# Declaring away the waits that other waits already imply, in a kernel that sums reciprocals

## The chip, the cores and the metric

The kernel runs on one core of one Trainium2 chip. The metric is the device time of one execution in microseconds (us). The input is 64 MiB of float32 in HBM, the output 64 KiB.

## The reference

```python
def setup_inputs():
    batch, seq, dim = 32, 512, 1024
    return {"x": np.abs(np.random.randn(batch, seq, dim)).astype(np.float32) + 1e-6}

def reference(x):
    return np.sum(1.0 / x, axis=-1).astype(np.float32)
```

There are 16384 rows of 1024 positive numbers. For each row the sum of the reciprocals is wanted.

## The kernel before

The 16384 rows are spread over the 128 partitions, 128 rows on each. In what follows "row r" (0 to 127) means row r of every partition at once: a block of 128 x 1024 numbers, 512 KB.

A reciprocal is taken as exp(-ln(v)) on ScalarE. To halve that work, the kernel splits a row into two halves a and b of 512 and takes only one reciprocal for each pair, q = 1/(a*b). Then 1/a + 1/b = (a + b) * q. A plan written out by hand, a list of tokens (PLAN), gives the order of all work; `tc.manual_schedule()` keeps each engine's instructions in that order. A token is a letter, a row, a count of rows (+2) and a place (@6):

- **D** (line 120): SyncE issues a load of the next n rows into the ring, a buffer in SBUF for 40 rows. There are 32 loads, the first nine of 8 rows, the last nine of one row. Loads take eight semaphores in turn.
- **P** (line 129): GpSimd multiplies the halves of one to three rows into a slot of `prod` (22 slots).
- **C** and **V** (lines 138 and 143): in place of P, TensorE copies the second half into a bank of PSUM with an identity matrix, and VectorE multiplies the halves. **W** (line 143) is the same product on VectorE with both halves read from SBUF.
- **S** (line 150): TensorE adds the halves into a PSUM bank, two matmuls with the identity, that the profile shows as four records.
- **L** (line 159): ScalarE takes ln of the slots, in place.
- **E** (line 167): ScalarE takes exp(-...), either in place in `prod` or into one or two PSUM banks (@).
- **R** (line 175): VectorE reduces. Where the row had an S, it multiplies q in `prod` (512) with the sum in PSUM and adds up. Otherwise it multiplies the row in the ring (1024) with q in PSUM, taken for both halves. A second, short instruction (DVE_READ_ACCUMULATOR2_ANT) writes the row's sum into `sums`.

At the end (line 195) SyncE stores `sums`.

The framework watches which instruction reads and writes which part of `ring`, `prod`, `ps` and `sums`, and sets semaphore waits for each dependence between engines. It knows what an engine has itself waited for, but not what that other engine had waited for before. An instruction carries one wait; further ones go into separate instructions in front of it on the same engine, which only wait (EVENT_SEMAPHORE in the profile). For example the reduce of row 0 waits for ScalarE, which wrote q into PSUM, and for GpSimd, which had read the row from the ring that the reduce overwrites. ScalarE had waited for GpSimd already, through `prod`.

The plan's last rows stand in this order: `S121@3 W121 R115 L119+3 P122 R118 S120@1 R117 E119+3 P123 R116 S124@4 L122+2 P124 R121 R120 E122+2 W125 S125@2 R119 L124+2 P126 R123 S126@0 E124+2 P127 R122 L126 R125 S127@1 E126 R124 L127 R126 E127 R127` (places left out where they do not matter). A little before come W117 and P118, neither of which needs the other.

Of the kernel before, what the change touches and what calls it, by code (L numbers as in the profile page):

```python
# [11 lines left out]
def kernel(  # L12
# [5 lines left out]
    nc = tc.nc  # L18
# [5 lines left out]
    R = 40  # L24
    NP = 22
    S = float(2**17)
# [41 lines left out]
    Ln = mybir.ActivationFunctionType.Ln  # L68
    Exp = mybir.ActivationFunctionType.Exp
# [34 lines left out]
    pslot = {r + j: b + j for op, r, n, b in ops if op == "L" for j in range(n)}  # L104

    def xs(r, h):
        return ring[:, r % R, h * H : (h + 1) * H]

    loaded = 0
    bank, copied, halves = {}, {}, set()  # L110

    with tc.manual_schedule():
        for op, r, n, b in ops:
            p = pslot.get(r)
            if op == "D":
                n, r = r, loaded
                while n:
                    a = r % R
                    m = min(n, R - a)  # L119
                    nc.sync.dma_start(  # L120
                        out=ring[:, a : a + m, :], in_=x_v[:, r : r + m, :]
                    )  # L122
                    r, n = r + m, n - m
                loaded = r  # L124
            elif op == "P":
                while n:  # L126
                    a, p = r % R, pslot[r]  # L127
                    m = min(n, R - a)
                    nc.gpsimd.tensor_tensor(  # L129
                        out=prod[:, p : p + m, :],  # L130
                        in0=ring[:, a : a + m, :H],
                        in1=ring[:, a : a + m, H:],
                        op=mult,
                    )
                    r, n = r + m, n - m
            elif op == "C":
                copied[r] = b
                nc.tensor.matmul(  # L138
                    ps[:, b, :], lhsT=ident, rhs=xs(r, 1), start=True, stop=True
                )  # L140
            elif op in "WV":
                in1 = xs(r, 1) if op == "W" else ps[:, copied[r], :]
                nc.vector.tensor_tensor(  # L143
                    out=prod[:, p, :], in0=xs(r, 0), in1=in1, op=mult
                )
            elif op == "S":
                bank[r] = b
                halves.add(r)
                for h in range(2):
                    nc.tensor.matmul(  # L150
                        ps[:, b, :],
                        lhsT=ident,
                        rhs=xs(r, h),
                        start=h == 0,
                        stop=h == 1,
                    )
            elif op == "L":
                pg = prod[:, p : p + n, :]
                nc.scalar.activation(out=pg, in_=pg, func=Ln, scale=S)  # L159
            elif op == "E":  # L160
                pg = prod[:, p : p + n, :]
                rc = pg
                if b is not None:
                    rc = ps[:, b : b + n, :]
                    for j in range(n):
                        bank[r + j] = b + j
                nc.scalar.activation(out=rc, in_=pg, func=Exp, scale=-1.0)  # L167
            elif op == "R":
                other = ps[:, bank[r], :]
                if r in halves:  # L170
                    row = prod[:, p, :]
                else:
                    row = ring[:, r % R, :].rearrange("p (h e) -> p h e", h=2)
                    other = other.unsqueeze(1).to_broadcast([P, 2, H])
                nc.vector.tensor_tensor_reduce(  # L175
                    out=row,
                    in0=row,
                    in1=other,
                    scale=S,
                    scalar=0.0,  # L180
                    op0=mult,
                    op1=add,
                    accum_out=sums[:, r : r + 1],
                )
            elif op == "X":
                row = ring[:, r % R, :]
                nc.scalar.activation(out=row, in_=row, func=Ln)
                nc.scalar.activation(
                    out=row,
                    in_=row,  # L190
                    func=Exp,
                    scale=-1.0,
                    accum_out=sums[:, r : r + 1],
                )
        nc.sync.dma_start(out=out_v, in_=sums)


# [28 lines left out]
```

## Time and profile before

| what | value |
|---|---|
| time, median of 4 runs | 171.75 us (171.58 to 172.11) |
| the profiled execution | 172.11 us, its span 170.1 us |
| TensorE matmul busy | 138.5 us (81%) |
| ScalarE busy | 131.1 us (77%) |
| VectorE busy | 130.4 us (77%) |
| GpSimd busy | 124.3 us (73%) |
| queue of the loads, share of 16 DMA engines over the span | 93.4% |
| read from HBM | 67.11 MB, 395 GB/s over the span |
| clock granted to TensorE, mean | 0.976 |

The span runs from the first to the last recorded instruction; the time of an execution also has what lies around it. In the profile's views L120 is line 120 of the kernel; PE is TensorE, PEld its weight loads, DVE is VectorE, ACT ScalarE, POOL GpSimd, SP SyncE, and a q behind the name (DVEq) is the engine's sequencer, that is its waiting instructions. The DMA view names each queue with its packets, megabytes and share; "instruction" packets are those that bring instructions to the engines.

### The profile page before, as it was taken

The page shows a single profiled execution, that of the slowest core. Times are in us where ns is not written, and L with a number is a line of the kernel's source. Part 1 is how long each engine was busy: PE and PEld are TensorE (multiplying, and loading weights), DVE is VectorE, ACT ScalarE, POOL GpSimd, SP SyncE. Part 2 cuts the span into 40 slices and gives each one's busy share as a digit, 9 for nine tenths or more (in the row PEclk, how much of TensorE's full clock was granted, in tenths as well). Part 3 has the DMA queues.
Part 4 walks back from the last instruction along what each step waited for, and adds up shares of the span by engine and source line. Part 5 has one row for each costly group of instructions (what it writes and reads, how often), then busy time and mean ns, then how long its engine had stood idle before and what let it go on. Part 6 is the DMA issues. An engine that isn't in the chain of part 4 may idle for free.

```text
span 170.1 us, 1382 instructions
## 1 busy us (share of the span) xinstructions
PE 138.5 (81%) x300; PEld 57.9 (34%) x300; DVE 130.4 (77%) x281; ACT 131.1 (77%) x133; POOL 124.3 (73%) x73
## 2 busy tenths in 40 slices
PE   0008999796995989779995999859999999898990
PEld 0003444242432434234342443224443444333340
DVE  0001777868886886868868689999999999999991
ACT  3002969969595996949789699988987999896990
POOL 1008969697995969779696999959919876974750
PEclk9999999999997899969999999999999999999998
DMA  6999999999999999999999999999999999999600
GB/s 216 401 470 393 462 401 447 416 447 416 424 433 424 439 424 435 433 432 439 424 439 405 418 420 433 443 409 424 435 416 428 420 425 427 408 409 408 252 4 17
DMA packets 4760, 67.26 MB, mean 395 GB/s; under 512 B 528, under 2 KB 656, under 8 KB 1808
## 3 DMA queue, kind: packets, MB, share of 16 engines
q1 hardware_dynamic: 4752, 67.18, 93.4%
q14 instruction: 6, 0.05, 0.1%
q8 instruction: 2, 0.03, 0.1%
HBM read 67.11 MB, written 0.07 MB: 395 GB/s over the span
## 4 chain that ended last, share of the span: by engine, by line
DMA 79%; ACT 7%; PE 4%; POOL 3%; issue 2%; DVE 1%; SPq 1%; POOLq 0%; DVEq 0%
DMA ring<-in_x_dram 79%; PE ps L150 4%; ACT prod L159 4%; POOL prod L129 3%; ACT ps L167 2%; SPq L120 1%; ACT prod L167 1%; DVE ring L175 1%; DVE prod L175 0%; DVE sums L175 0%; POOLq L129 0%; DVEq L175 0%; DVEq L221 0%
## 5 line engine op out<-in xcount | busy, mean ns | idle before, releaser
L129 POOL TENSOR_TENSOR prod<-ring 128x1024 f32<-128x1024 f32 (+1 forms) x67 | 123.6, 1874 | 39.2 <-DMA ring<-in_x_dram 32.6
L150 PE MATMUL ps<-ring,ident 128*128 128x512 f32 x268 | 121.8, 607 | 3.7 <-DMA ring<-in_x_dram 3.3
L159 ACT ACTIVATE prod<-prod 128x1024 f32<-128x1024 f32 (+2 forms) x66 | 67.1, 1020 | 30.8 <-POOL prod L129 29.9
L175 DVE CUSTOM_DVE_ANT_1 ring<-ring,ps 128x1024 f32<-128x1024 f32 x61 | 72.2, 1217 | 16.4 <-ACT ps L167 16.1
L150 PEld LDWEIGHTS ps<-ring,ident 128*128 128x128 f32 x268 | 52.0, 196 | 73.3 <-issue 60.9
L175 DVE CUSTOM_DVE_ANT_0 prod<-prod,ps 128x512 f32<-128x512 f32 x67 | 43.4, 682 | 1.0 <-ACT prod L167 0.5
L138 PE MATMUL ps<-ring,ident 128*128 128x512 f32 x32 | 20.0, 715 | 24.0 <-DMA ring<-in_x_dram 23.4
L167 ACT ACTIVATE prod<-prod 128x1024 f32<-128x1024 f32 (+2 forms) x34 | 35.4, 1042 | 0.9
L167 ACT ACTIVATE ps<-prod 128x1024 f32<-128x1024 f32 (+2 forms) x32 | 31.5, 985 | 2.4 <-DVE sums L175 1.5
L143 DVE TENSOR_TENSOR prod<-ring,ps 128x512 f32<-128x512 f32 x16 | 10.9, 684 | 19.4 <-PE ps L138 19.2
L138 PEld LDWEIGHTS ps<-ring,ident 128*128 128x128 f32 x32 | 5.9, 212 | 34.3 <-issue 15.9
L175 DVE DVE_READ_ACCUMULATOR2_ANT sums<- 128x1 f32 x128 | 10.5, 82 | 0.0
L143 DVE TENSOR_TENSOR prod<-ring 128x512 f32<-128x512 f32 x9 | 8.2, 928 | 0.0
L77 ACT ACT_TABLE_LOAD x1 | 1.3, 1283 | 0.7 <-PEq L210 0.7
masks.py:197 POOL MEMSET ident<- 128x128 f32 x1 | 0.2, 205 | 0.3 <-POOLq L210 0.3
masks.py:199 POOL TENSOR_SCALAR_AFFINE_SELECT ident<-ident 128x128 f32<-128x128 f32 x1 | 0.3, 295 | 0.1
L210 POOL MEMSET const-float32-0.0<- 128x1 f32 x1 | 0.1, 99 | 0.2 <-issue 0.2
L210 POOL MEMSET const-bfloat16-1.0<- 128x1 bf16 x1 | 0.1, 102 | 0.0
L210 POOL MEMSET const-uint8-127<- 128x1 uint8 x1 | 0.1, 102 | 0.0
L210 POOL MEMSET const-float32-1.0<- 128x1 f32 x1 | 0.1, 99 | 0.0
## 6 DMA issues: line engine op xcount, KB each, us to landing
ring<-in_x_dram SPq DMA_DIRECT2D x9, 4096.0 KB, 38.5
ring<-in_x_dram SPq DMA_DIRECT2D x7, 1536.0 KB, 35.5
ring<-in_x_dram SPq DMA_DIRECT2D x2, 2560.0 KB, 36.7
ring<-in_x_dram SPq DMA_DIRECT2D x9, 512.0 KB, 15.9
ring<-in_x_dram SPq DMA_DIRECT2D x1, 3072.0 KB, 35.6
ring<-in_x_dram SPq DMA_DIRECT2D x3, 1024.0 KB, 29.4
ring<-in_x_dram SPq DMA_DIRECT2D x1, 2048.0 KB, 36.7
out_dram<-sums SPq DMA_DIRECT2D x1, 64.0 KB, 1.6
```

The costliest lines, as they stand in the source:

```text
L77: nc.scalar.add_instruction(mybir.InstLoadActFuncSet(name=nc.get_next_instruction_name(), act_func_set_id=act_sets.index("natural_log_exp_ ...
L120: nc.sync.dma_start(out=ring[:, a : a + m, :], in_=x_v[:, r : r + m, :])
L129: nc.gpsimd.tensor_tensor(out=prod[:, p : p + m, :], in0=ring[:, a : a + m, :H], in1=ring[:, a : a + m, H:], op=mult,)
L138: nc.tensor.matmul(ps[:, b, :], lhsT=ident, rhs=xs(r, 1), start=True, stop=True)
L143: nc.vector.tensor_tensor(out=prod[:, p, :], in0=xs(r, 0), in1=in1, op=mult)
L150: nc.tensor.matmul(ps[:, b, :], lhsT=ident, rhs=xs(r, h), start=h == 0, stop=h == 1,)
L159: nc.scalar.activation(out=pg, in_=pg, func=Ln, scale=S)
L167: nc.scalar.activation(out=rc, in_=pg, func=Exp, scale=-1.0)
L175: nc.vector.tensor_tensor_reduce(out=row, in0=row, in1=other, scale=S, scalar=0.0, op0=mult, op1=add, accum_out=sums[:, r : r + 1],)
L210: nc = _bacc.Bacc("TRN2", target_bir_lowering=False, num_devices=1)
```

## The change

Each issued operation is handed to a new function, `note`, with the spaces it reads and writes: rows of the ring, slots of `prod`, banks of PSUM. `note` keeps for each operation a clock: how far each other engine is known to have come when this operation begins. The operations that must come before a new one are looked at from the latest on. One that the clock already covers is declared to be no dependence; for the others the clock is raised by what the earlier operation itself knew. The order of the instructions and their work stay as they are. The store of `sums` is not noted.

```diff
+    history = {}
+    begun = {}
+    count = {}
+
+    def note(engine, inst, reads=(), writes=()):
+        inst = inst.ins
+        known = dict(begun.get(engine, {}))
+        before = {}
+        for spaces, writing in ((reads, False), (writes, True)):
+            for space in spaces:
+                for other in history.get(space, ()):
+                    if writing or other[3]:
+                        before[other[0].name] = other
+        needed = sorted(before.values(), key=lambda o: -o[4])
+        for other in needed:
+            o_inst, o_engine, o_tick, _, _, o_known = other
+            if o_tick <= known.get(o_engine, 0):
+                tc.declare_no_dep(inst, o_inst, reason="implied by other waits")
+                continue
+            if o_engine == engine:
+                continue
+            for e, t in o_known.items():
+                known[e] = max(known.get(e, 0), t)
+            known[o_engine] = max(known.get(o_engine, 0), o_tick)
+        count[engine] = count.get(engine, 0) + 1
+        begun[engine] = known
+        entry = (engine, count[engine])
+        if engine == "SP":
+            entry = (f"load {count[engine]}", 1)
+        for spaces, writing in ((reads, False), (writes, True)):
+            for space in spaces:
+                history.setdefault(space, []).append(
+                    (inst, *entry, writing, sum(count.values()), known)
+                )
...
-                    nc.sync.dma_start(
+                    inst = nc.sync.dma_start(
                         out=ring[:, a : a + m, :], in_=x_v[:, r : r + m, :]
                     )
+                    note("SP", inst, writes=rows(r, m))
...
-                    nc.gpsimd.tensor_tensor(
+                    inst = nc.gpsimd.tensor_tensor(
...
+                    note("POOL", inst, rows(r, m), slots(r, m))
...
-                nc.vector.tensor_tensor_reduce(
+                inst = nc.vector.tensor_tensor_reduce(
...
+                note(
+                    "DVE",
+                    inst,
+                    [("bank", bank[r])],
+                    slots(r, 1) if r in halves else rows(r, 1),
+                )
```

C, V, W, S, L and E are noted in the same way.

More of the change, by code (lines that the diff above doesn't have):

```diff
@@ L110, with rows, slots @@
     bank, copied, halves = {}, {}, set()
+    history = {}
[31 more added lines that the diff above has]
+                )
+    def rows(r, n):
+        return [("row", q % R) for q in range(r, r + n)]
+    def slots(r, n):
+        return [("slot", pslot[q]) for q in range(r, r + n)]
     with tc.manual_schedule():
@@ L137 @@
                 copied[r] = b
-                nc.tensor.matmul(
+                inst = nc.tensor.matmul(
                     ps[:, b, :], lhsT=ident, rhs=xs(r, 1), start=True, stop=True
                 )
+                note("PE", inst, rows(r, 1), [("bank", b)])
             elif op in "WV":
                 in1 = xs(r, 1) if op == "W" else ps[:, copied[r], :]
-                nc.vector.tensor_tensor(
+                inst = nc.vector.tensor_tensor(
                     out=prod[:, p, :], in0=xs(r, 0), in1=in1, op=mult
                 )
+                other = [("bank", copied[r])] if op == "V" else []
+                note("DVE", inst, rows(r, 1) + other, slots(r, 1))
             elif op == "S":
@@ L149 @@
                 for h in range(2):
-                    nc.tensor.matmul(
+                    inst = nc.tensor.matmul(
                         ps[:, b, :],
@@ L156 @@
                     )
+                    note("PE", inst, rows(r, 1), [("bank", b)])
             elif op == "L":
                 pg = prod[:, p : p + n, :]
-                nc.scalar.activation(out=pg, in_=pg, func=Ln, scale=S)
+                inst = nc.scalar.activation(out=pg, in_=pg, func=Ln, scale=S)
+                note("ACT", inst, writes=slots(r, n))
             elif op == "E":
@@ L166 @@
                         bank[r + j] = b + j
-                nc.scalar.activation(out=rc, in_=pg, func=Exp, scale=-1.0)
+                inst = nc.scalar.activation(out=rc, in_=pg, func=Exp, scale=-1.0)
+                if b is None:
+                    note("ACT", inst, writes=slots(r, n))
+                else:
+                    banks = [("bank", b + j) for j in range(n)]
+                    note("ACT", inst, slots(r, n), banks)
             elif op == "R":
@@ L184 @@
                 )
+                note(
[4 more added lines that the diff above has]
+                )
             elif op == "X":
                 row = ring[:, r % R, :]
-                nc.scalar.activation(out=row, in_=row, func=Ln)
-                nc.scalar.activation(
+                inst = nc.scalar.activation(out=row, in_=row, func=Ln)
+                note("ACT", inst, writes=rows(r, 1))
+                inst = nc.scalar.activation(
                     out=row,
@@ L194 @@
                 )
+                note("ACT", inst, writes=rows(r, 1))
         nc.sync.dma_start(out=out_v, in_=sums)
```

## The prediction

> **What bounds the kernel now.** I read the page's DMA table first, then the chain of work that ended last near its end, then the busy time by stretches.
>
> ```profile
> q1 hardware_dynamic: 4752, 67.18, 93.4%
> q14 instruction: 6, 0.05, 0.1%
> q8 instruction: 2, 0.03, 0.1%
> ...
> DMA 79%; ACT 7%; PE 4%; POOL 3%; issue 2%; DVE 1%; SPq 1%; POOLq 0%; DVEq 0%
> ```
>
> The loads fill the queue: 67 MB, and the stretches from 5 to 155 us all show a DMA share of 0.99 to 1.03. What the compute engines save while the queue is full only makes them wait longer for the next row. So the question is what the end looks like. The chain from 140 us on:
>
> ```profile
> 145.51 13.56 DMA ring<-in_x_dram
> 159.08 0.04 issue
> 159.12 7.15 PE ps L150 x16
> 166.27 0.03 issue
> 166.30 0.02 DVEq L175
> 166.32 0.08 issue
> 166.40 0.69 DVE prod L175
> ```
>
> Row 124 lands at 159.08. TensorE then forms the sums S124, S125, S126, S127, each four records 0.429 us apart, without a gap: 7.15 us. The last reduce R127 takes 0.69 and ends at 167.09. Writing out the result and the closing barrier take 3.0 more, to 170.09. The profiled execution took 172.11 us, 2.02 more than its span; the median of the four runs is 171.75, 0.36 below it. I make the sum in the profiled execution and take the difference to the median.
>
> ```profile
> core 0: us, PE busy (x) PEld busy (x) DVE busy (x) ACT busy (x) POOL busy (x), PEclk, DMA share, GB/s
> ...
> 150.00:155.00 5.00, 4.64 (x11) 1.58 (x9) 5.00 (x10) 3.85 (x5) 2.75 (x3) 1.00 1.03 408
> 155.00:160.00 5.00, 4.58 (x10) 1.93 (x11) 5.00 (x13) 4.54 (x4) 3.67 (x4) 1.00 0.96 383
> 160.00:165.00 5.00, 5.00 (x13) 2.28 (x12) 5.00 (x14) 4.88 (x7) 3.02 (x3) 1.00 0.06 26
> ```
>
> VectorE is busy through all of the last 15 us too. In the timeline it finishes R126 at 165.98 and idles only 0.41 us before R127. So two things close together set the end: row 124's landing plus 7.15 on TensorE, and VectorE's list.
>
> **The change, part by part.** No operation and no order changes. The compiled programs hold fewer instructions that only wait: VectorE 82 to 24, GpSimd 45 to 26, SyncE 46 to 39, TensorE 21 to 17, ScalarE 46 to 46.
>
> *What a waiting instruction costs.* Where ScalarE's end releases a full-row reduce on VectorE, the reduce starts 0.143 us later if a separate wait stands before it (the chain at 71.43: 0.03 issue, 0.02 wait, 0.09 issue), and 0.032 later in the two places where it waits itself. So 0.11 us for each stall. The waits view counts 18 such stalls; 18 x 0.11 = 2.0 us of VectorE's idle time. Between stalls the waits are hidden: reduces follow each other at 1.14 or 0.61 us whether one stands between or not. The 2.0 us are covered by the loads before 155 us. If that cover were gone they would be worth up to 2.0. After the last such stall, at 147.6, VectorE runs 0.11 earlier, but W121 waits for row 121 (landed 155.24) and takes it back. On the last TensorE chain the separate waits at 160.4 and 161.6 lie inside running matmuls; they cost nothing and stay. SyncE issues loads earlier by 0.05 at most, with 11 us or more of queued loads ahead of them: nothing. Taken alone, then, this is worth 0, with bounds 0 and 2.0; the value is 0 because TensorE's last chain starts at a landing.
>
> *What fewer instructions do to the loads.* The DMA queues also carry the instructions:
>
> ```profile
> q1 hardware_dynamic: 109, 0.39, 100.6%
> q14 instruction: 1, 0.01, 2.1%
> ```
>
> This is the DMA view of 152 to 153 us: beside 109 packets of the loads, one packet of instructions (8192 bytes, begun at 152.34, 0.34 us). During the span such packets begin at 46.82, 69.85, 96.61, 103.41 and 152.34, and one at 169.93 after all work; two of 16384 bytes, on q8, at 66.49 and 134.20. Each load raises its semaphore 16 times, once for each DMA engine, and the rows can be used when the last has come. From first to last of the 16 it is 0.76 to 0.85 us for the loads landing from 13 to 43 us, 1.17 at 53, 2.0 at 73, 2.0 to 2.1 up to 151.7, and 3.06 for row 120, the first load that lands after the packet at 152.34. It stays at about 3.0 up to row 127 (159.84 to 162.82). So that one packet put one DMA engine, already among the three slowest, 1.0 us further back, and every one of the last eight rows lands 1.0 us later for it. Row 124 among them starts the chain above.
>
> Whose packet is it? VectorE had begun 70 instructions at 46.82, 198 at 103.41 and 322 at 152.34: steps of 128 and 124. The three packets also alike took 342, 333 and 339 ns, the other two 309 each; and after 46.82 and 103.41 it is an engine well back that moves (to 1.17, then from 1.13 to 2.03). ScalarE at those times stands at 39, 100 and 161, GpSimd at 32, 73 and 110, SyncE at 16, 43 and 71: no equal steps that fit. So I take them as VectorE's, one for each 128 instructions, the third due at about 326. VectorE recorded 366 instructions; 58 fewer is 308. The third packet then never comes. GpSimd's and ScalarE's single ones stay, some later. The slowest DMA engines are then those at 2.0 to 2.1, so the last eight rows land 3.06 - 2.04 = 1.02 us earlier.
>
> [...]
>
> *What is late next.* Row 124 lands at 158.06. TensorE must be free: S121 now waits until row 121 lands (155.24, then 154.22) and S120 for R115, and by their spacing S120 ends near 157.9. S124 to S127 then run from 158.10 to 165.25, R127 from 165.38. VectorE: from W121's start to R126's end it took 155.26 to 165.98, 10.72 us; from 154.23 that is 164.95, before 165.25. ScalarE ends E127 at 165.87 - 1.02 = 164.85. All follow, so the end moves by the whole 1.02: span 169.07, profiled 171.09, median 171.75 - 1.02 = 170.73.
>
> One condition stands in it:
>
> ```profile
> 149.33 2.51 POOL L129 TENSOR_TENSOR prod<-ring 128x512 f32<-128x512 f32 x2
> ...
> 150.62 1.77 DVE L143 TENSOR_TENSOR prod<-ring 128x512 f32<-128x512 f32 x1
> ```
>
> W117 took 1.77 us; seven of the nine products of this kind (both operands in SBUF) took 0.69. GpSimd had begun a product 0.05 us before it (P118, 150.58). The other slow one, at 109.35, also began 0.05 after a GpSimd product; and where W began first (130.81), GpSimd's product took 1.80 instead of 1.28. So whoever begins first holds the other off. With the 0.11 saved at 147.6, W117 begins at 150.51, before P118, and VectorE gains 1.08 us. Alone this is worth nothing, since W121 waits for its row; with the earlier rows it is what lets VectorE follow.
>
> **The rivals.** *A, forecast: the third packet is gone and W117 goes first.* -1.02, 170.73. Chance 0.60.
>
> *B: the packet is gone, W117 still loses to P118.* The margin is only 0.07 us. VectorE then reaches W121 at about 155.15, is done with R126 near 165.85, and R127 starts there instead of 166.40: -0.5, 171.25. Chance 0.10.
>
> *C, slower: a GpSimd product overtakes W125.* With W117 late, W125 starts at about 160.5. P126, which waited for row 126 until 161.65, may start at 160.62 once that row is 1.02 earlier. From the point where W125 comes behind it, W125 waits 1.15 us for GpSimd, and seven reduces stand behind it: R127 starts near 167.05, +0.65, 172.4. For it: the two meet within 0.15 us. Against it: W117's release would put W125 a whole us ahead. Chance 0.10.
>
> *D: the last rows land as before.* The packet is another engine's (ScalarE, whose count does not change, stands at 161), or it is sent by another rule. Then S124 starts at 159.12 and the saved waits lie behind the loads: 0, 171.75. Against it are the steps of 128. Chance 0.20.
>
> **How the numbers follow.** The likeliest case gives 170.73. About 0.2% (0.34 us) is what a measurement of this kernel tells from no change. Faster: A and B, 0.70, and 0.02 of D for part of the 2.0 us showing after all: 0.72. Slower: C, 0.10. Same: 0.18. A, B and D hold 0.90, and the four runs reach 0.17 below their median, the unprofiled ones no more than that apart; the range goes from 170.73 - 0.35 to 171.75 + 0.1, 170.4 to 171.85. A's own range is 170.4 to 171.1.
>
> **What would show it.** In the profile after: no instruction packet on q14 between about 125 and 165 us; the 16 landings of the last loads within 2.1 us; DMA until about 158.1 in the chain, then TensorE 7.15; W117 at 0.69; stalls of VectorE on ScalarE shorter by 0.11 each while the span up to 150 us is unchanged. A packet of instructions near 152 us, or S124 near 159.1, would make it wrong; so would a product W125 of 1.8 us.

## The result and the profile after

The changed kernel takes 170.33 us (median of ten executions, 170.24 to 170.60 and one of 172.05), the kernel before 171.76 in the same comparison (14 executions, 171.58 to 172.11). The ratio is 0.9927 with a 95% interval of 0.9908 to 0.9946: 1.4 us faster. Nearly half of the executions of either kernel are some 3 us longer; wherever one of these was profiled, a stretch of 3.4 us at half the granted TensorE clock lay near 112 us, and here and below I use of them only landings, packets of instructions and SyncE's closing, no times.

The profiled execution took 170.38 us, its span 168.4; before 172.11 and 170.1. I read the same views as before. First the page's DMA queues:

```profile
q1 hardware_dynamic: 4752, 67.18, 94.2%
q8 instruction: 2, 0.03, 0.1%
q14 instruction: 4, 0.03, 0.0%
```

The loads are the same to the packet; q14 carries four packets of instructions where it carried six. They begin at 51.16, 69.30, 112.08 and 121.79 us in the trace. One more, at 170.05, comes after all work and lies behind the end of the span; the one of this kind before, at 169.93, still lay within it and is the sixth. So one packet during the work is gone. None comes between 125 and 165 us. The DMA view of 152 to 153 us, where one stood before, has only loads:

```profile
q1 hardware_dynamic: 115, 0.41, 103.6%
```

The chain of work that ended last, from 145 us on:

```profile
145.27 12.63 DMA ring<-in_x_dram
157.90 0.04 issue
157.95 7.15 PE ps L200 x16
165.09 0.03 issue
165.12 0.02 DVEq L232
165.14 0.08 issue
165.23 0.69 DVE prod L232
```

It is the same chain piece by piece (line 200 is S, 232 is R). Only the landing of row 124 moved, from 159.08 to 157.90, and what follows it came along: R127 starts at 165.23 instead of 166.40, 1.18 us earlier. From first to last of the 16 landings of one load it is 2.17 to 2.29 us for the last eight rows; before it was 2.98 to 3.07. Of the 1.18 us, then, 0.78 come with the last of the 16 parts (row 124: 3.07 and 2.29 us behind the first); the other 0.40 are in the first part already, and they stand there well ahead of the packet (rows 117 and 118: first part at 148.34 before, 147.95 now).

The busy time by stretches shows what the earlier rows did to the other engines:

```profile
core 0: us, PE busy (x) PEld busy (x) DVE busy (x) ACT busy (x) POOL busy (x), PEclk, DMA share, GB/s
150.00:155.00 5.00, 4.89 (x12) 2.00 (x11) 4.75 (x10) 4.53 (x6) 3.37 (x3) 1.00 1.03 409
155.00:160.00 5.00, 4.94 (x12) 2.01 (x11) 5.00 (x13) 4.78 (x4) 3.77 (x3) 1.00 0.91 365
160.00:165.00 5.00, 5.00 (x12) 1.90 (x10) 4.81 (x13) 4.56 (x7) 2.52 (x2) 1.00 0.04 16
```

VectorE, busy all 5.00 us of the first stretch before, now has gaps in it. That is W117, in VectorE's timeline:

```profile
150.27 0.69 DVE L191 TENSOR_TENSOR prod<-ring 128x512 f32<-128x512 f32 x1
150.88 1.22 DVE L232 CUSTOM_DVE_ANT_1 ring<-ring,ps 128x1024 f32<-128x1024 f32 x1
```

It took 0.69 us instead of 1.77. GpSimd's P118 began 0.085 us after it, at 150.356, and took 1.74 in its turn.

One more thing moved that the prediction had taken as unchanged. From R127's start to the end of the span it took 3.69 us before and takes 3.15 now. Together: 1.18 + 0.54 = 1.72, the whole difference of the two spans (170.09 and 168.38). The medians are 1.43 apart: the profiled execution before was 0.35 above its median.

### The profile page after: what moved, and what is told of

Its sections match the earlier page's. It is cut to its first block, busy times and chain, and to the rows that moved or that the text cites. A ratio compares the mean times of both kernels' runs of the same rounds, so it can differ in the third digit from the quotient of the medians.

```text
span 168.4 us, 1294 instructions
## 1 busy us (share of the span) xinstructions
PE 138.4 (82%) x300; PEld 57.9 (34%) x300; DVE 129.3 (77%) x281; ACT 131.1 (78%) x133; POOL 124.7 (74%) x73
## 3 DMA queue, kind: packets, MB, share of 16 engines
q1 hardware_dynamic: 4752, 67.18, 94.2%
## 4 chain that ended last, share of the span: by engine, by line
DMA 80%; DVE 6%; PE 4%; ACT 4%; POOL 3%; issue 1%; SPq 0%; DVEq 0%; POOLq 0%
DMA ring<-in_x_dram 80%; DVE ring L232 5%; PE ps L200 4%; POOL prod L175 3%; ACT ps L219 2%; ACT prod L210 1%; DVE prod L232 1%; DVE sums L232 0%; SPq L165 0%; DVEq L232 0%; POOLq L175 0%; DVEq L286 0%
## 5 line engine op out<-in xcount | busy, mean ns | idle before, releaser
L191 DVE TENSOR_TENSOR prod<-ring 128x512 f32<-128x512 f32 x9 | 7.2, 820 | 0.2 <-DMA ring<-in_x_dram 0.2
```

The costliest lines, as they stand in the source:

```text
L191: inst = nc.vector.tensor_tensor(out=prod[:, p, :], in0=xs(r, 0), in1=in1, op=mult)
```

## The experiments

**Theory.** The third packet of VectorE's instructions goes out over one of the DMA engines that bring the last rows; without it they land earlier, and TensorE's last chain starts earlier. **Rival.** The waits themselves cost the time, on whichever engine they stand; the packet is a bystander. After the first results came a second question: where the 0.54 us of the closing come from.

All edits are to the changed kernel.

### VectorE alone

```diff
-                tc.declare_no_dep(inst, o_inst, reason="implied by other waits")
+                if engine == "DVE":
+                    tc.declare_no_dep(inst, o_inst, reason="implied by other waits")
```

Only VectorE's implied waits are declared away; it records 308 instructions as in the changed kernel. SyncE, which keeps all its waits, records 86 (before 83).

> Waits are declared away on VectorE alone (58 fewer instructions there, 308 recorded; GpSimd and TensorE as before; SyncE, which is left undeclared, has three more waits). Theory (VectorE's third packet of instructions is gone): no packet near 152 us, row 127 lands within 2.3 us of its first sixteenth, about 161.6, the last reduce starts near 165.2, 1.0 to 1.4 us faster than the kernel before. Rival (the time came from cheaper waits on GpSimd, SyncE and TensorE): within 0.3 us of the kernel before.

No time comes of this run (173.61 to 173.69 us). Its trace: no packet on q14 between 125 and 165 us, 2.27 us from first to last of the 16, row 127 at 161.66 (161.61 in the changed kernel). Run again:

> The first experiment once more (waits declared away on VectorE alone), because a stretch of half clock on TensorE fell at 112 us there and hid the end. Theory: without it, 1.0 to 1.4 us faster than the kernel before; rival: within 0.3 us of it.

170.28, 170.36 and 170.42 us, ratio 0.992 (0.9902 to 0.9938); row 127 at 161.43. The DMA view of 150 to 165 us has only loads:

```profile
q1 hardware_dynamic: 1085, 3.92, 65.4%
```

VectorE alone gives the whole gain, the closing's share too: it is 3.19 us here (more on that below). What TensorE and GpSimd save can be kept or left.

### All but VectorE

```diff
-                tc.declare_no_dep(inst, o_inst, reason="implied by other waits")
+                if engine != "DVE":
+                    tc.declare_no_dep(inst, o_inst, reason="implied by other waits")
```

VectorE keeps its 366 instructions.

> Waits are declared away on every engine but VectorE (366 recorded there as before, SyncE 76, GpSimd 108). Theory: the packet near 152 us is still there, row 127 lands near 162.8 with about 3.0 us between first and last sixteenth, the last reduce starts near 166.2 to 166.4; only the 0.54 us that the closing lost less can be gained, so 0 to 0.6 us faster than before. Rival (cheaper waits everywhere): about half or more of the change's 1.4 us.

Again no time comes of it (174.12 to 174.43 us). A packet begins at 154.28, when VectorE has begun 321 instructions; 2.96 us from first to last, row 127 at 162.68. Run again:

> The second once more (waits declared away on every engine but VectorE), for the same reason. Theory: without the half clock at 112 us, 0 to 0.6 us faster than the kernel before, all of it behind the last reduce; rival: half of the change's gain or more ahead of the last reduce.

171.05, 171.09 and 171.24 us, ratio 0.9965 (0.9948 to 0.9983), 0.76 above the changed kernel. The packet begins at 151.83, VectorE again at 321. The DMA view of 151.5 to 152.5 us, then the chain:

```profile
q1 hardware_dynamic: 111, 0.41, 104.0%
q14 instruction: 1, 0.01, 2.1%
```

```profile
145.16 13.41 DMA ring<-in_x_dram
158.57 0.04 issue
158.61 7.15 PE ps L201 x16
165.76 0.03 issue
165.79 0.02 DVEq L233
165.81 0.08 issue
165.89 0.69 DVE prod L233
```

With the packet, row 124 lands at 158.57 instead of 157.90, and R127 comes 0.66 later. But the closing is 3.16 here, as short as in the changed kernel. So this kernel has one of the two gains, the closing, without the other, the landing; that is where its 0.67 us on the median of the kernel before (0.60 in this run's own comparison) come from, nearly all. By the two profiles R127 is also 0.51 earlier than in the kernel before (165.89 and 166.40), which the expectation did not have: the loads in the profiled execution before were late as a whole. The first part of row 127 came at 159.84 there, and at 159.35 to 159.72 in the thirteen other profiles.

### Bringing the packet back without a wait

```diff
+    junk = pool.tile([P, 64], f32)
...
+        for j in range(60):
+            nc.vector.memset(junk[:, j : j + 1], 0.0)
```

60 short instructions are added ahead of the plan, writing a column that nobody reads. They begin 28 ns apart and are done by 2.5 us; no wait is added. VectorE records 368.

> The changed kernel with 60 memsets of one column ahead of VectorE's first product, where it idles for 13 us anyway: 368 recorded instructions, none of them a wait. Theory (the count of VectorE's instructions decides): a third packet near 145 to 155 us is back, one DMA engine is 3 us behind, row 127 lands about 1.0 us later than in the changed kernel, which becomes 0.9 to 1.1 us slower, though every wait is still gone. Rival (the waits themselves were the cost): as fast as the changed kernel, within 0.2 us.

171.25, 171.47 and 171.54 us: 0.9 to 1.2 slower for 1.7 us of work at the very start. The DMA view of 149 to 150 us:

```profile
q1 hardware_dynamic: 105, 0.40, 102.6%
q14 instruction: 1, 0.01, 2.0%
```

Three packets come when VectorE has begun 62, 182 and 321 instructions, the third at 149.17; 2.67 us from first to last, row 124 at 158.62 (0.72 later than in the changed kernel), row 127 at 162.37. In this execution (171.47) VectorE was also late by 1.6 us from W117 on and its list ended the chain, so not all of its surplus is the landing's. Run again:

> The third experiment once more (60 memsets more on VectorE), because the half clock on TensorE fell at 113 us there. Theory: the third packet near 149 us, the last rows 0.7 to 1.1 us later than in the changed kernel, the last reduce as much later, time 0.7 to 1.1 us over the changed kernel's 170.3. Rival (waits were the cost): within 0.2 us of 170.3.

171.07 and 171.13 us, 0.74 and 0.80 above the changed kernel. In the profiled execution, which is not one of these two, the third packet begins at 149.60 (VectorE at 319); 3.02 us from first to last, row 127 at 162.47. This is the rival's end: no wait was added, and the time is back.

The same with `range(12)`, which makes 320 instructions, not enough for a third packet:

> The same with 12 memsets: 320 recorded instructions, short of the 326 at which the third packet was due. Theory: no third packet before the loads end, as fast as the changed kernel within 0.2 us. Rival (memsets or a shifted second packet cost by themselves): slower than the changed kernel by a share of what 60 cost, 0.2 us.

170.19 and 170.34 us. The profiled execution has no third packet until all work is done, 2.06 us from first to last, row 127 at 161.51. Its DMA view of 150 to 165 us:

```profile
q1 hardware_dynamic: 1096, 3.96, 66.1%
```

So it is not the added instructions as such.

And with `range(30)`, 338 instructions, so that the third packet comes when the rows that matter have landed:

> The changed kernel with 30 memsets ahead of VectorE's first product: 338 recorded. Theory: the third packet comes back, but only when VectorE has begun 321 instructions, near 159 to 161 us; row 124 has landed by then (about 157.9), the rows 126 and 127 may land up to 1.0 us later, and TensorE does not wait for them, so the kernel is as fast as the changed one within 0.3 us. Rival (a third packet costs 1.0 us wherever it comes): 0.9 to 1.1 us slower than the changed kernel, as with 60.

170.25 us in the one execution whose time can be used. The profiled one is another (173.56 us); its DMA view of 160.5 to 161.5 us has the packet, begun at 161.01, when VectorE had begun 309 instructions, among the last dozen packets of the loads:

```profile
q1 hardware_dynamic: 12, 0.04, 9.1%
q14 instruction: 1, 0.01, 2.0%
```

Row 124 had landed at 157.78; only row 127 was touched (2.40 us from first to last, 161.75), and it is not what TensorE's chain waits for first. So a packet at 161 leaves row 124 alone. That it costs no time is not shown: the execution of 170.25 us lies within the changed kernel's own range, but it has no profile, and when its packet came is not known. (In the profile of the changed kernel VectorE begins its 279th instruction, which is the 309th here, at 156.44 us, and its 292nd at 161.76.)

### One wait kept

```diff
-                tc.declare_no_dep(inst, o_inst, reason="implied by other waits")
+                if (op, r) != ("R", 109):
+                    tc.declare_no_dep(inst, o_inst, reason="implied by other waits")
```

One waiting instruction stays ahead of R109, a reduce not long before W117. VectorE records 309.

> The changed kernel, but the reduce R109 keeps its waits, so that one waiting instruction more stands before it at 147.4 us; 309 recorded on VectorE, no third packet. Theory of the holding off: R109 starts 0.11 us later, W117 begins at about 150.38, just behind GpSimd's P118 at 150.36, and takes 1.7 us instead of 0.69; W125 starts near 160.3, still ahead of P126; the last reduce starts 0.3 to 0.5 us later than in the changed kernel (rival B of the prediction), or, if W125 falls behind P126, 1.5 us later (rival C). If the order stays (the margin is 0.02 us): as the changed kernel. Rival (one waiting instruction costs its own 0.11 us at most): within 0.15 us of the changed kernel with W117 at 0.69 or at 1.7.

170.56 and 170.62 us, ratio 0.9934 (0.9913 to 0.9955). No third packet, row 127 at 161.49. The kept wait shows at its place: R109 starts 0.130 us behind the end of the exp that releases it, against 0.033 in the changed kernel and 0.143 in the kernel before. And W117 now began 0.022 us behind P118 (150.234 against 150.212) and lost:

```profile
150.23 1.80 DVE L192 TENSOR_TENSOR prod<-ring 128x512 f32<-128x512 f32 x1
151.96 1.21 DVE L233 CUSTOM_DVE_ANT_1 ring<-ring,ps 128x1024 f32<-128x1024 f32 x1
```

R113 to V119 start 1.08 us later than in the changed kernel, W121 to R126 0.75: in the changed kernel VectorE waits for a row ahead of W121, and a third of a us is taken up there. Another half of a us is taken up ahead of R127, for which VectorE waits there too. The chain now ends in VectorE's list, no longer in TensorE's:

```profile
164.33 0.60 DVE prod L233
164.93 0.01 DVE sums L233
164.94 0.32 DVE prod L233
165.26 0.21 issue
165.47 0.08 DVE sums L233
```

R127 starts at 165.47, 0.25 later than in the changed kernel (expected were 0.3 to 0.5). So this is case B of the prediction, made on purpose: by the two profiles it costs 0.25 us. The times alone would not show it: 170.56 and 170.62 lie at the upper end of the changed kernel's 170.24 to 170.60.

### Where the closing's 0.54 us come from

In the kernel before SyncE, which stores the result and then takes part in the closing barrier, stands still for 0.41 us between two DRAINs (instructions of that barrier) that follow each other within 0.06 us in the changed kernel. The second DRAIN then takes 0.13 us instead of 0.01; with 0.05 us in two gaps ahead of it, that is nearly the whole 0.54. SyncE records 83 instructions before, 76 now. To bring the count back, and nothing else, SyncE's waits are declared for the first 16 loads only:

```diff
-                tc.declare_no_dep(inst, o_inst, reason="implied by other waits")
+                if engine != "SP" or count.get("SP", 0) < 16:
+                    tc.declare_no_dep(inst, o_inst, reason="implied by other waits")
```

> The changed kernel, but SyncE declares waits away only up to its 15th load, so that SyncE has as many instructions as in the kernel before (83 recorded). The profiled execution before spent 3.69 us from the start of the last reduce to the end, the one after 3.15. If SyncE's count made that difference: 3.6 to 3.7 here and 0.5 us slower than the changed kernel. If it was that one execution's own: 3.15 and as fast as the changed kernel within 0.2 us.

83 instructions, and the 0.41 us are back at the same place: closing 3.69, with R127 0.12 *earlier* than in the changed kernel (165.11). 170.69, 170.78 and 171.16 us, 0.45 above the changed kernel by the medians, and 0.54 - 0.12 = 0.42 by the two profiles. Beside it the kernel before once more, for a second profile of its closing:

> The kernel before, profiled a second time. If the 3.69 us from the last reduce to the end belong to the kernel, they come again; if to that one execution, 3.15. The third packet should come again when VectorE has begun 321 or 322 instructions, and row 124 land at 159.1 within 0.3 us.

Closing 3.69 again (no time comes of its one execution, 174.62 us). Its third packet begins at 153.87, VectorE at 321, 2.99 us from first to last, row 127 at 162.42. Row 124 landed at 158.71, 0.37 earlier than in the first profile and outside the 0.3 expected. The first parts of its last eight rows land within 0.05 us of those in the changed kernel: the 0.40 us found above belonged to that one execution, and neither to the kernel nor to the packet.

With VectorE alone SyncE records 86, more than before, and yet the closing is 3.19. Its 0.41 us are there too, three instructions earlier in the list's order: ahead of the wait for the store, which then takes 0.61 instead of 1.00. Counted from the front it is the same instruction each time, the 80th recorded. A last run puts another step of the closing there, with `< 19` in place of `< 16`, 81 instructions:

> SyncE's loads are declared only up to the 19th, so that SyncE records 81 instructions (before 83, after 76). In every profile so far in which SyncE records 80 or more, its 80th starts about 0.41 us late with nothing in front of it that the profile shows: with 83 recorded (before, its repetition, and the kernel with the first 16 loads declared) that is the second DRAIN of the closing, and the end comes 3.69 us after R127's start; with 86 recorded it lies ahead of the wait for the store and costs nothing (3.19). Theory (the place is fixed in SyncE's list of instructions): the 0.41 us stand ahead of the last DRAIN but are partly in place of nothing, so the closing takes 3.15 + 0.41 - 0.07 = 3.5 us; both first DRAINs follow each other within 0.1 us. Rival (it belongs to the DRAINs, whenever SyncE waits more often): the gap stands again ahead of the second DRAIN, 3.69. Rival (chance of a single execution): no gap, 3.15. The rest as after: no third packet of VectorE, row 127 landing near 161.6, time 170.5 to 170.8 if undisturbed.

| kernels | recorded by SyncE | its 80th | idle ahead of it, us | R127's start to the end, us |
|---|---|---|---|---|
| before (two profiles), first 16 loads declared | 83 | second DRAIN | 0.41 | 3.69 |
| VectorE alone (two profiles) | 86 | wait for the store | 0.41 | 3.19 |
| first 19 loads declared | 81 | last DRAIN | 0.44 | 3.44 |
| changed kernel and the seven others of its count | 76 | none | none | 3.14 to 3.22 |

The stop moved with the count, to the last DRAIN, and the first two follow each other within 0.05 us. So it belongs to a place in SyncE's instructions, not to a DRAIN. (The whole took 171.06 us in its one execution, above the 170.5 to 170.8 expected: W117 lost to P118 here as well, 1.41 us, and R127 came at 165.61.) What SyncE does in these 0.4 us the trace doesn't show: no instruction packet lies in them, in the kernel with the first 16 loads declared the next one begins at 168.62, after the stop has ended. That stays open.

## Why the prediction was right, point by point

**Which engine's packet, and whether it goes: right, and shown.** It went with VectorE's count alone, stayed with it, came back with 60 instructions that wait for nothing, and stayed away with 12 as long as there was work. Wherever a third packet came, VectorE had begun 309 to 322 instructions. The prediction had "about 326". Its reading of the counts was weaker than it says: ScalarE's 39, 100 and 161 are equal steps too, of 61, more equal than VectorE's 128 and 124. The experiments settle it: in the changed kernel ScalarE begins its 161st instruction at 151.5 us and no packet comes, and with 60 more instructions on VectorE the packet comes when ScalarE stands at 156 and 154.

**What the packet costs the loads: right in kind, a little over-sized, and the close match of the profiles is luck.** It was read as 1.02 us from two stretches of one execution. Row 124 came 1.18 earlier, but 0.40 of that was the lateness of the one profiled execution before, and 0.78 was the packet's. Over the executions with a third packet (six: 162.31 to 162.82) and without (seven: 161.43 to 161.66) row 127 lands 0.65 to 1.4 us apart, 0.96 on the mean (162.51 and 161.55); the difference of first and last landing is 2.92 and 2.14 on the mean, 0.78 apart. The profiled execution before was the latest of the first six. It was also 0.35 us above its kernel's median, and that is about the surplus: all but VectorE, with the packet and the short closing, is 0.76 above the changed kernel. The landing is thus worth some 0.8 to 0.9 us on the medians; 1.43 measured less 0.54 for the closing gives 0.89. The packet itself takes 0.34 us; why one part of every later row falls back by two to three times as much, no run shows. Nor does a trace name a DMA engine beside a packet or a landing: that each of the 16 landings of a load is one engine's, and that the packet goes over one of these engines, is the author's reading of the one landing in 16 that falls back (row 124 in the kernel before: the last 3.07 us behind the first, the one ahead of it 2.03).

**TensorE's chain, VectorE and ScalarE follow: right.** S124 was forecast for 158.10 and started at 157.95, R126's end for 164.95 (164.80), E127's for 164.85 (164.70), R127 for 165.38 (165.23). All four are 0.15 early, as row 124 is: it came 1.18 earlier, not 1.02.

**W117 goes first: right by 0.085 us, and this was luck of a narrow kind.** The margin forecast was 0.07. The 0.11 us of the forecast are there (R109 0.033 instead of 0.143 behind its release). One wait more in front (0.022 us behind P118), or another's rhythm, turns it. The price of losing was the weak term: case B was put at half the gain (-0.5 from before, R127 near 165.85), and R127 came at 165.47, 0.25 us behind the changed kernel. The loss of 1.08 us on W117 is taken up for the most part by two waits that VectorE has in the changed kernel anyway, ahead of W121 and of R127.

**Case C did not come in any profile whose time is used.** The nearest to it were those where W117 was late: W125 stayed ahead of P126 by 0.18 us with 60 more instructions and with the first 19 loads declared, by 0.20 with the one wait kept (160.154 and 160.350), and took 0.68. In three of the profiles that give no time (the first of all but VectorE, the second of 60 more instructions, the kernel before again) W125 did take 1.56 to 1.60 us.

**The waits themselves: 0 of the end, right.** From 140 to 150 us VectorE starts 0.30 to 0.35 us earlier than in the profile before, but the rows land 0.2 to 0.3 earlier there too, and all but VectorE, which keeps VectorE's 82 waits, begins W117 at 150.269, the changed kernel at 150.271. Apart from W117's place in front of P118, the end takes nothing of the waits, since the landing of row 124 starts the last chain. The kernel with all but VectorE took 30 such instructions off other engines and gained only at the closing.

**The step that was missing: the closing.** The prediction carried it as "3.0 more", the same for both. It saw only its sum, after R127's end, and not what was in it: 0.41 us in which SyncE waits for nothing that the trace shows. The forecast of the median, 170.73, is 0.40 above the 170.33 measured; the closing's 0.54 less the over-sized landing make that. Without the closing the changed kernel would stand near 170.8, as the kernel with SyncE's count of before does.

**VectorE itself paid nothing that shows.** It ran on past the packet without a gap (5.00 us busy from 150 to 155 us with it, in the kernel before), but the rows paid 0.8 us or so. Its packets of instructions are 8192 bytes each and come 128 and 124 recorded instructions apart in the kernel before, 113 in the changed kernel (at 66 and 179), 120 and 139 with 60 more instructions.

## What to carry to other kernels

When the DMA queues are full (the loads took 94.2% of the DMA engines' time over the span here) and the end hangs on the last landing, count instructions as traffic: look in the DMA view for instruction packets ahead of the last landings, find whose they are by the counts of instructions begun, and see whether the engine can be kept below that count (309 to 322 for VectorE's third packet here), by fewer waits or by fewer operations. Read a late landing by its 16 parts, since one late part holds the whole row (0.78 us here). And compare the closing of two profiles, piece by piece, before the difference of two times is given to the one term that was looked for.

## What the runs showed of the hardware that was not expected

SyncE stops for 0.41 to 0.44 us ahead of its 80th recorded instruction, in all six profiles in which it has one (81, 83 and 86 instructions). It costs 0.3 to 0.5 us where nothing else is waited for, and nothing where it falls ahead of a wait that is long anyway.

60 instructions that begin 28 ns apart at the start of the kernel, over by 2.5 us, cost 0.7 to 1.2 us at its end.

A lead of 0.085 us or a lag of 0.022 us of one product on another decides over 1.1 us of one instruction (0.69 or 1.80), and then over 0.25 us of the end. What makes the later of the two take longer (GpSimd's took 1.74 us where it came second), no run shows.
